# An FFN down projection as one level of Strassen, a finer weight ring and moved seams, in a layer bound by TensorE

## The chip, the cores and the metric

The kernel runs on all 8 cores of one Trainium2 chip (two dies of four cores). Each core computes one batch element of 8192 tokens; the cores exchange nothing. The metric is the device time in microseconds (us) of the slowest core. Such a program has two states, whatever the kernel: in many executions the cores of one die, sometimes of both, show a lower granted TensorE clock, and the time is some per cent to 18% longer. Everything below compares fast executions with fast executions, or undisturbed dies with each other. "Typical core" means the median over the cores of one profiled execution; it is some 10 us below the slowest core.

## The reference

The layer is a macaron: half a SwiGLU FFN, a mixer, half a second FFN, then a final norm. The FFNs hold most of the arithmetic. `D_MODEL` is 1024, `D_FF` is 2816, `SEQ` 8192.

```python
def swiglu_ffn(x, w_gu, w_down):
    gate, up = jnp.split(x @ w_gu, 2, axis=-1)
    return (jax.nn.silu(gate) * up) @ w_down

for l in range(DEPTH):        # DEPTH = 1
    x = x + 0.5 * swiglu_ffn(rms_norm(x, ffn1_norm_g[l]), ffn1_w_gu[l], ffn1_w_down[l])
    x = x + hybrid_mixer(rms_norm(x, mix_norm_g[l]), ...)   # mLSTM branch, pooling branch, gated merge
    x = x + 0.5 * swiglu_ffn(rms_norm(x, ffn2_norm_g[l]), ffn2_w_gu[l], ffn2_w_down[l])
return rms_norm(x, final_norm_g)
```

## The kernel before

The tokens go through in 16 tiles of 512. Step s issues two FFNs, the second FFN of tile s-1 and the first FFN of tile s+1 ("F2" and "F1" below), and weaves the mixer of tile s into them. One such step is called a round. Matmuls are bf16; the activations lie with channels on the partitions and tokens along the free axis. Before the rounds there are three stretches that fill the pipeline: F1 of tile 0, F1 of tile 1 (with the first mixer), F2 of tile 0. I call them the start.

The down projection makes 8 output chunks of 128 channels, each as 22 matmuls of 512 tokens that accumulate in one PSUM bank, and one eviction on VectorE (DVE), which reads the sum from PSUM and adds it to `x`:

```python
def down(j, part):
    def run():
        s = ringF.use(p0 + 11 + j)
        w = wF[s]
        ...
        for k in range(part * 11, part * 11 + 11):
            mm(PS(b), w[:, k * 128:(k + 1) * 128], hid[:, k, :], k == 0, k == NFC - 1)
        if part == 1:
            stt(x[:, j, :], PS(b), 0.5, x[:, j, :], ALU.mult, ALU.add)
            ringF.release()
    return run
```

All weights stream from DRAM for every tile through a ring of four slots of 4096 columns. The first use of a piece comes as fp32 through a casting transfer; the bf16 copy is stored right away to a scratch in DRAM, from the queue of SyncE (SP), and later tiles load that copy:

```python
if k not in converted:
    converted.add(k)
    dma("pool", ch_c[s], w[:, 0:n], wsrc_d[k][:, 0:n], ...)      # fp32 -> bf16 on the way
    ...
    dma("sp", ch_s[s], scr_d[k][:, 0:n], w[:, 0:n], ...)          # keep the bf16 copy
else:
    ...
    dma("sp", ch_w[s], w[:, 0:n], scr_d[k][:, 0:n], ...)
```

The seams between tiles: the final norm of the tile before is put among the first units of the next FFN, and the mixer ends with the norm that feeds the next F2:

```python
un.insert(4 + 2 * q, p)                # final-norm units, from the 4th unit on
...
norm_rs(1, 0, "M")
norm_xn(xnF, x, G2, 0, range(KC))      # eight scalings in one go
...
interleave(main, side, 0.0, 0.95)
```

A small recorder derives every wait from the tiles that an operation reads and writes, so a buffer that is used twice brings its wait with it, and DMAs of one channel wait for each other.

The softmax here doesn't subtract the row's maximum and nothing guards it: scores larger than these inputs give would overflow.

## Time and profile before

| fast executions | us |
|---|---|
| before, 16 executions in all | median 5482.8; the fast ones 5476 to 5484 |
| typical core of the profile | 5469.6 |
| of this: the three stretches of the start | 228.6 + 241.4 + 179.1 (sum on the typical core 647.6) |
| the rounds in the middle (14 F1 and 13 F2) | 4465.8; one round is 174.5 (F1) + 155.5 (F2) = 330.0 |
| the last two F2 | 356.3 |

The stretches are cut where the matmuls pass from the down projection of one FFN to the gate/up projection of the next. The lines of the profile that carry the argument stand in the prediction. How to read it: the tenths show by slices when an engine was busy; the windows show the same in microseconds for chosen stretches; the waits say for whom PE (TensorE) stood still. PE is TensorE (PEld its weight loads), DVE is VectorE, ACT ScalarE, POOL GpSimd, SP SyncE. Of the names, `hid` is the FFN's hidden layer, `x` the residual stream, `xnF` and `xnM` the normalised inputs of FFN and mixer, `accb` the sum of squares for a norm, `ys`, `tF`, `Cf` and `sm` buffers of FFN and mixer, `wF` and `wM` the weight rings, `wsrc` the fp32 weights, `scr` and `scrD` the scratches in DRAM.

### The profile page before, as it was taken

To read this page: it belongs to the slowest core of one execution; us is meant where nothing else is said; L and a number is where in the kernel's file an instruction comes from. 1 tells how busy PE (TensorE), PEld (TensorE's weight loads), DVE (VectorE), ACT (ScalarE), POOL (GpSimd) and SP (SyncE) were. 2 spreads that over 40 slices of the span, in tenths; PEclk is the share of its full clock that TensorE was granted. 3 is DMA by queue.
4 is the path that set the end of the run, shared out by engine and by line. 5 is a ranking of instruction groups with operands and counts; after the bars stand their busy time and mean duration, and the time that the engine had idled before them with its cause. 6 is when DMAs were issued, how large, how long until landed. Compare 5 with 4: busy or idle time off the path is not lost.

```text
span 5481.8 us, 74964 instructions; the slowest of 8 cores (5458.8 to 5481.8 us)
## 1 busy us (share of the span) xinstructions
PE 5262.0 (96%) x25751; PEld 2425.4 (44%) x25751; DVE 2063.0 (38%) x3028; ACT 1694.5 (31%) x2979; POOL 1003.4 (18%) x967
## 2 busy tenths in 40 slices
PE   6688999999999999999999999999999999999998
PEld 2243444444444444444444444444444444444443
DVE  1243424444343343424444243343434434243432
ACT  1223323333232333323333232332423333233322
POOL 0212312112120221202112120221302112120210
PEclk9899999999999999999999999999999999999999
DMA  9969944444434444444544434444444444434433
GB/s 201 216 163 210 223 165 146 173 155 173 158 139 176 153 171 152 151 165 150 179 155 167 156 138 172 157 173 152 146 172 148 176 158 154 169 139 158 151 129 138
DMA packets 145122, 894.89 MB, mean 163 GB/s; under 512 B 16240, under 2 KB 18416, under 8 KB 79600
## 3 DMA queue, kind: packets, MB, share of 16 engines
q1 hardware_dynamic: 136400, 842.07, 43.8%
q0 software_dynamic: 7632, 47.19, 5.6%
q8 instruction: 215, 3.52, 0.3%
q14 instruction: 155, 1.27, 0.1%
q10 hardware_dynamic: 720, 0.84, 0.1%
HBM read 855.43 MB, written 81.79 MB: 171 GB/s over the span
## 4 chain that ended last, share of the span: by engine, by line
PE 81%; DMA 7%; DVE 5%; ACT 3%; issue 3%; POOL 1%; DVEq 0%; ACTq 0%; SPq 0%; POOLq 0%
PE ps L329 80%; DVE xnF L357 3%; DMA wF<-wsrc 2%; ACT L350 2%; DMA scr<-wF 2%; DVE x L357 1%; DMA wM<-wsrc 1%; ACT rs L350 1%; DMA wM<-scr 1%; DMA x<-pb 1%; PE ps L333 0%; POOL accb L353 0%; ACT sqt L350 0%; ACT tM L350 0%; DVE Cf L353 0%
## 5 line engine op out<-in xcount | busy, mean ns | idle before, releaser
L329 PE MATMUL ps<-xnF,wF 128*128 128x512 bf16 x11264 | 2579.1, 380 | 37.5 <-ACT tF L350 13.0
L329 PEld LDWEIGHTS ps<-xnF,wF 128*128 128x128 bf16 x11264 | 1099.1, 98 | 1367.8 <-issue 77.2
L329 PE MATMUL ps<-hid,wF 128*128 128x512 bf16 x5632 | 1270.9, 380 | 38.1 <-DMA wF<-wsrc 38.1
L353 DVE TENSOR_TENSOR hid<-tF,ps 128x512 bf16<-128x512 f32 x704 | 481.5, 686 | 1693.1 <-PE ps L329 1497.7
L329 PE MATMUL ps<-xnM,wM 128*128 128x512 bf16 x4096 | 971.6, 381 | 38.4 <-DVE ys L357 25.8
L353 POOL TENSOR_TENSOR acc<-acc,sqt 128x512 f32<-128x512 f32 x378 | 494.2, 1311 | 2742.7 <-ACT sqt L350 2736.1
L329 PEld LDWEIGHTS ps<-hid,wF 128*128 128x128 bf16 x5632 | 546.2, 98 | 675.0 <-issue 45.2
L350 ACT ACTIVATE tF<-ps 128x512 f32<-128x512 f32 x704 | 418.4, 596 | 1263.5 <-PE ps L329 1210.2
L329 PEld LDWEIGHTS ps<-xnM,wM 128*128 128x128 bf16 x4096 | 401.0, 98 | 521.2 <-issue 49.8
L357 DVE SCALAR_TENSOR_TENSOR x<-ps,x 128x512 f32<-128x512 f32 x384 | 264.6, 689 | 743.4 <-PE ps L329 740.5
L350 ACT ACTIVATE sqt<-x 128x512 f32<-128x512 f32 x441 | 270.0, 625 | 776.1 <-DVE x L357 620.8
L350 ACT ACTIVATE tM<-ps,pvh 128x512 f32<-128x512 f32 x320 | 219.9, 687 | 773.6 <-PE ps L329 773.6
L357 DVE SCALAR_TENSOR_TENSOR tM<-zy,pv_s,tM 128x512 f32<-128x512 bf16 x384 | 294.2, 767 | 197.2 <-POOL tM L365 155.4
L350 ACT ACT_TABLE_LOAD x223 | 286.1, 1283 | 129.8 <-PE ps L329 104.5
L357 DVE SCALAR_TENSOR_TENSOR tB<-tM,ps 128x512 bf16<-128x512 f32 x256 | 176.0, 688 | 239.2 <-PE ps L329 239.1
L357 DVE SCALAR_TENSOR_TENSOR xnF<-x,pv_s,rs 128x512 bf16<-128x512 f32 x256 | 205.1, 867 | 117.9 <-ACT rs L350 117.9
L329 PE MATMUL ps<-qkT,wM 128*128 128x512 bf16 x1024 | 242.7, 381 | 5.4 <-DMA wM<-wsrc 5.4
L365 POOL TENSOR_SCALAR tM<-zy,pv_s 128x512 f32<-128x512 bf16 x128 | 92.8, 728 | 666.3 <-ACT zy L350 607.7
L329 PEld LDWEIGHTS ps<-qkT,wM 128*128 128x128 bf16 x1024 | 100.5, 98 | 127.9 <-issue 8.3
L350 ACT ACTIVATE zy<-ps,pv_s 128x512 bf16<-128x512 f32 x128 | 87.6, 684 | 199.2 <-PE ps L329 199.2
L329 PE MATMUL ps<-wM,xnM 128*128 128x512 bf16 x512 | 122.1, 382 | 13.1 <-DMA wM<-scr 13.1
L329 PE MATMUL ps<-poolT,wM 128*128 128x512 bf16 x512 | 131.4, 379 | 0.0
(82 smaller groups left out, 2244.2 us busy)
## 6 DMA issues: line engine op xcount, KB each, us to landing
wF<-scr SPq DMA_DIRECT2D x330, 1024.0 KB, 4.9
wF<-scr SPq DMA_DIRECT2D x240, 704.0 KB, 4.2
wM<-scr SPq DMA_DIRECT2D x105, 1024.0 KB, 5.9
wM<-scr SPq DMA_DIRECT2D x120, 768.0 KB, 4.5
out<-x SPq DMA_DIRECT2D x64, 512.0 KB, 3.7
x<-x SPq DMA_DIRECT2D x15, 2048.0 KB, 12.7
wF<-wsrc POOLq DMA_DIRECT2D x22, 1024.0 KB, 16.4
scr<-wF SPq DMA_DIRECT2D x22, 1024.0 KB, 15.3
```

Of the source, the lines that this page charges most:

```text
L329: P.op("pe", lambda e: e.matmul(out, lhsT, rhs, start=start, stop=stop), reads=[lhsT, rhs], writes=[out])
L350: P.op("act", lambda e: e.activation(out, in_, func, **kw), reads=rd, writes=wr)
L353: P.op(eng, lambda e: e.tensor_tensor(out, in0, in1, op), reads=[in0, in1], writes=[out])
L357: P.op("dve", lambda e: e.scalar_tensor_tensor(out, in0, scalar, in1, op0, op1), reads=rd, writes=[out])
L365: P.op(eng, lambda e: e.tensor_scalar(out, in0, s1, s2, op0, op1), reads=rd, writes=[out])
```

## The change

The intent is to take arithmetic from PE, which is 96% busy. It has three parts that come together.

1. **Strassen.** The down projection is cut in halves by output chunks (4 and 4), by contraction chunks (11 and 11) and by tokens (256 and 256), and done with seven products, m1 to m7, instead of eight. Most products take sums or differences of quarters of the weights or of `hid` as inputs. DVE makes the token-side sums. The weight-side sums are made once, at tile 0 of each FFN, which itself is computed plainly, and are stored in a new scratch `scrD` that later tiles load.
2. **Ring.** Four slots of 4096 columns become 16 of 1024, so pieces of different sizes follow each other densely. The converted weights of tile 0 are stored after use, no longer right after the cast.
3. **Seams.** The final norm comes 16 units later, the mixer starts 3% later, the eight scalings are spread, two projections of the mixer move behind the mLSTM part, and some buffers are shared to make room.

```diff
-NF = 4
+SUB = 1024
+NSUBF = 16
+PROD = ("m2", "m1", "m5", "m3", "m6", "m4", "m7")
...
-        hid = sb("hid", [128, NFC, T], BF16)
-        wF = [sb(f"wF{i}", [128, 4096], BF16) for i in range(NF)]
+        hid = sb("hid", [128, 5, KH, TH], BF16)      # 4 quarters and one for sums
+        wF = sb("wF", [128, NSUBF * SUB], BF16)
...
+        ch_sF = [P.dma_chan(f"sF{q}") for q in range(4)]
...
+                            if not first:
+                                ringF.release((which, i, "gu", g))
+                                tt(q5(4, g, g + 1), q5(0, g, g + 1), q5(3, g, g + 1), ALU.add)
...
+                def conv_put(n):
+                    ...
+                    for q, pr in enumerate(PROD):
+                        o = st["sum", n, pr]
+                        dma("sp", fch(ch_sF, "s"), scrD_d[...], o, ...)
...
+                EV = {"m1": ((0, 0, 0.5), (1, 1, 0.5)), "m2": ((1, 0, 0.5), (1, 1, -0.5)), "m5": ((0, 1, 0.5), (0, 0, -0.5)),
+                      "m3": ((0, 1, 0.5),), "m6": ((1, 1, 0.5),), "m4": ((1, 0, 0.5),), "m7": ((0, 0, 0.5),)}
+                RHS = {"m2": 0, "m1": 4, "m5": 3, "m3": 4, "m6": 1, "m4": 0, "m7": 2}
+
+                def product(q, pair, mi):
+                    ...
+                        if mi == 0 and pr not in ("m6", "m7"):
+                            st["b", pair] = bank("F")     # m6, m7 accumulate on the bank of m3, m4
+                        b = st["b", pair]
+                        for k in range(KH):
+                            mm(PS(b, mi * TH, (mi + 1) * TH), ringF.col(pc, (mi * KH + k) * 128), hid[:, RHS[pr], k, :], ...)
+                        if mi == 1:
+                            for bot, hf, sc in EV[pr]:
+                                v = xq(4 * bot + 2 * pair, hf)
+                                stt(v, PS(b)..., sc, v, ALU.mult, ALU.add)
...
+                sums = (tsum(4, 1, 3, ALU.subtract) + tsum(1, 0, 1, ALU.add) +
+                        tsum(0, 2, 0, ALU.subtract) + tsum(2, 2, 3, ALU.add))
+                for q in range(7):
+                    for pair in range(2):
+                        for mi in range(2):
+                            down.append((1.2, product(q, pair, mi)))
+                            if q >= 2 and pair == 0 and sums:
+                                down.append((0.0, sums.pop(0)))
...
-            @u(0.3)
-            def _():
-                norm_rs(1, 0, "M")
-                norm_xn(xnF, x, G2, 0, range(KC))
+            us.append((1.5, lambda: norm_rs(1, 0, "M")))
+            for k in range(KC):
+                us.append((0.6, lambda k=k: norm_xn(xnF, x, G2, 0, [k])))
...
-                        un.insert(4 + 2 * q, p)
+                        un.insert(20 + 2 * q, p)
...
-                interleave(main, side, 0.0, 0.95)
+                interleave(main, side, 0.03, 0.95)
```

Cut from the diff: the ring class and its loaders, the sums of the weights at tile 0, the shared buffers, the moved projections and the host's layout of the weights.

## The prediction

> **What bounds the kernel now.** I read the per-core view first, then the head of the page, the chain of waits, PE's waits, the groups by shape, the timeline and the windows. All cores agree within 0.4% at a granted clock of 0.988 to 0.991, so this profile (5481.8 us) is the fast state; the medians of the two dies differ by 10 us. The quoted 5591.58 us is a median over two fast and two slow executions and is not my base: everything below is fast against fast.
>
> ```profile
> span 5481.8 us, 74964 instructions; the slowest of 8 cores (5458.8 to 5481.8 us)
> PE 5262.0 (96%) x25751; PEld 2425.4 (44%) x25751; DVE 2063.0 (38%) x3028; ACT 1694.5 (31%) x2979; POOL 1003.4 (18%) x967
> PE   6688999999999999999999999999999999999998
> DMA  9969944444434444444544434444444444434433
> PE 81%; DMA 7%; DVE 5%; ACT 3%; issue 3%; POOL 1%; DVEq 0%; ACTq 0%; SPq 0%; POOLq 0%
> ```
>
> PE carries the span. DVE has room on average. The first five slices are different: DMA is full there and PE is not.
>
> ```profile
> L329 PE MATMUL ps<-hid,wF 128*128 128x512 bf16 x5632 | 1270.9, 380 | 38.1 <-DMA wF<-wsrc 38.1
> L357 DVE SCALAR_TENSOR_TENSOR x<-ps,x 128x512 f32<-128x512 f32 x384 | 264.6, 689 | 743.4 <-PE ps L329 740.5
> L353 DVE TENSOR_TENSOR qkT<-tB 128x512 bf16<-128x512 bf16 x128 | 54.4, 425 | 14.0 <-DVE tB L357 0.9
> 2639.78 2.54 PE L329 MATMUL ps<-xnF,wF 128*128 128x512 bf16 x11
> 316.27 0.39 PE L329 MATMUL ps<-qkT 128*128 128x128 bf16 x4
> 316.49 0.39 PE L333 MATMUL ps<-cbf,qkT 128*128 128x128 bf16 x4
> ```
>
> The 380 ns is a latency, not a cost: eleven 512-wide matmuls take 2.54 us, so each new one costs (2.54 - 0.38)/10 = 216 ns. Four 128-wide ones start every 0.22 us, 55 to 56 ns each, with new weights every time. Pricing all matmuls of the groups so (23,623 bf16 of 512 columns at 215.8 ns, 1,536 of 128 or 130 at 56.5, the small rest 20 us) gives 5,205 us. The other 277 us is PE waiting or running cold. The windows tell where; I cut them where the timeline passes from hid matmuls to xnF matmuls, which is where one FFN ends.
>
> ```profile
> 0.00:230.60 230.60, 138.42 (x553) 57.44 (x553) 38.52 (x58) 36.06 (x57) 33.88 (x46) 0.87 0.95 211
> 478.80:658.90 180.10, 159.41 (x807) 73.66 (x805) 77.59 (x110) 61.92 (x121) 53.86 (x61) 0.95 0.98 218
> 1648.30:1822.80 174.50, 171.09 (x804) 77.67 (x803) 61.10 (x96) 44.36 (x66) 18.10 (x14) 1.00 0.50 175
> 1822.80:1978.30 155.50, 154.77 (x808) 73.18 (x807) 67.25 (x94) 61.62 (x120) 42.96 (x43) 1.00 0.40 143
> ```
>
> After the span the columns are busy time of PE, weight loads, DVE, ACT, POOL, then granted clock, DMA share, GB/s. Counting the same prices per window: the first FFN holds 108 us of waits, the stretch to 478.8 another 37, the first F2 25; one steady round (both middle rows) is 330.0 us and holds about 5; the last two FFNs 31. So 170 us at the start, some 13 x 5 = 65 us in the steady part, 31 at the end.
>
> ```profile
> PE ps L329 <- DMA wF<-wsrc: 40.5, 5, 17.5
> PE ps L329 <- DVE x L363: 28.7, 3, 25.0
> PE ps L329 <- DVE ys L357: 25.8, 14, 2.3
> PE ps L329 <- POOL accb L353: 15.5, 15, 3.4
> PE ps L329 <- ACT tF L350: 13.4, 15, 1.0
> ```
>
> Waits seen about 15 times are once per round; those seen 3 or 5 times are the start.
>
> **What the Trainium skill says.** (1) "TensorE: Matmul & The Clock Gate", section "Wait — 56ns, not 53.3ns?": a warm stream starts a matmul every N/2.4 ns plus about 2.5 ns. This trace agrees at N = 512 (216) and 128 (56); at N = 256 it gives 109.2 ns, an estimate from that page, as no 256-wide matmul exists here. (2) "VectorE: DVE Perf Modes", "The perf-mode tier table": bf16 tensor_tensor in SBUF makes two elements a cycle, and any fp32 PSUM operand falls to one; its preceding errata section has a fixed term of 151 cycles at 0.96 GHz. The trace agrees: (512/2 + 151)/0.96 = 424 ns against 425, and 689 ns from PSUM. (3) "SBUF — State Buffer", "Who interferes with whom": DVE operations with two SBUF inputs contend with GpSimd operations that read SBUF. The trace has a related sign: the cast Cbf<-Cf takes 431 to 1316 ns for one shape. (4) The first page again, its peak-current warning under "Seeing it yourself": a die of busy cores can be held at 13/16 of the clock. This fast profile doesn't show it; whether it explains the slow executions stays open.
>
> **The change part by part.** The down projection becomes one level of Strassen: halves of 4 output chunks, 11 contraction chunks and 256 tokens, seven products instead of eight. That removes arithmetic from the bound engine.
>
> PE. An FFN's down part was 8 x 22 = 176 matmuls x 215.8 ns = 37.98 us. It becomes 7 x 4 x 11 = 308 of 256 columns x 109.2 ns = 33.63 us. The fixed part eats some of the eighth: 4.35 us is saved instead of 4.75. Tile 0 of each FFN stays plain while it makes the weight combinations, so 30 of 32 FFNs gain: 30 x 4.35 = **-130 us**. All of it is on the path in the steady part.
>
> DVE. Evictions go from 8 to 20 per FFN: 12 x 0.69 = 8.3 us. Four token-side sums of 2816 bf16 columns, each split 1536 + 1280: (768+151)/0.96 + (640+151)/0.96 = 0.96 + 0.82 us, four times = 7.1 us. Eleven sums of 256 columns in the gate/up part: 11 x 0.29 = 3.2 us. Together 18.6 us x 30 = 560 us, plus two sets of weight sums (estimate: 40 sums of 640 or 768 columns, about 0.53 us, 21 us each). DVE goes from 2063 to about 2660 us, half of the span. Not on the path by sum, but it bunches: a product is 44 x 0.109 = 4.8 us of PE, some 7.5 us with mixer work between. Its evictions (up to 4 x 0.69) and one sum (1.8) fill 2.4 to 4.6 us of that before the mixer's own DVE work. Where eight xnF scalings (0.75 each) land in the same stretch, DVE falls behind. Estimate: 0.5 us of PE stall per Strassen FFN, **+15 us**.
>
> DMA. Down weights go from 8 x 704 KB to 14 x 704 KB per FFN: 30 x 4.1 MiB = 130 MB more loads, and 9 MB more stores; 895 becomes about 1030 MB, 194 GB/s. The start already ran at 218 GB/s, and a load lands in 4.2 us with five pieces ahead: hidden in the steady part.
>
> Seams. Final-norm work moves from after the 4th to after the 20th unit; the mixer starts 3% later; the xnF scalings are spread. That should remove the accb wait (1 us a round) and part of the tF, hid and xnF waits (together about 2). The ys wait stays: its transposes still take all four mixer banks, and two pooling outputs now sit between them on DVE. Net **-20 us**.
>
> Start. Stores of converted gate/up weights no longer sit on SP's queue ahead of the pooling matrix, whose load was issued at 52.2 us and cost PE a 25 us wait: most of that goes. Against it, a slot is held until used and stored, and tile 0's down weights need sums on DVE, then 56 small stores per FFN; each sum waits for the previous store to leave the shared scratch. With DMA at 0.95 to 0.98 busy in the first and third windows, I expect -15 in F1 and +10 in F2: **-5 us**. End: xnF earlier, a two-chunk tail instead of one: **-3 us**.
>
> Sum: -130 + 15 - 20 - 5 - 3 = -143; 5481.8 - 143 = 5339, taken as 5335.
>
> **The rivals.** (a) DVE becomes the local bound in the down parts. For: the bunching above, and slowdown beside POOL, whose adds already take 1.3 us; a collision can add about 0.9 us (431 against 1316). Against: 50% on average, four banks that let PE run two products ahead. If each Strassen FFN lost 3 us instead of 0.5, 75 us of the gain goes: 5410. (b) Short matmuls lose to their weight loads. For: twice the loads per column, 98 ns each against 109. Against: 128-wide ones keep 56 ns with such a load each, so the loads overlap. At 120 ns per matmul the saving would be only 1.0 us per FFN: about 5440. (c) The start gets longer: the chain sum, store, sum on tile 0 costs 40 to 60 us more in two DMA-full stretches: about 5385. (d) The seam repairs work fully and the pooling wait goes whole: 65 + 25 us of present waits shrink to 20: about 5285.
>
> **Range and chances.** The PE saving is nearly arithmetic (122 to 141 us at 110 to 108 ns). The start is uncertain by 25 us, the DVE stalls by 25, the seams by 15; together about 38 us. Eight in ten: 5270 to 5410. The 2% line lies at 0.98 x 5481.8 = 5372, one such width above the estimate; (a), (b) and (c) lie beyond it. Faster 0.77, same 0.20, slower 0.03.
>
> **What would show it.** Right: 9,240 hid matmuls of 256 columns starting every 109 ns; a steady round near 320 us instead of 330.0; DVE near 2660 us; no accb wait; no 25 us gap before 84 us; about 1030 MB. Wrong: PE waits on DVE's hid sums or x evictions of over 1 us a round (a); a pace of 115 ns or more (b); the first three windows together above 659 us (c). A round that gets shorter by over 14 us would mean that the seams held more than I counted.

## The result, and the profile after

The changed kernel is correct. Ten executions gave a median of 5498.1 us; the fast ones took 5397 to 5416. The ratio of fast runs is 0.986, with a 95% interval of 0.985 to 0.988: 1.4% faster, which is within the 2% that count as the same. Ratios here are the mean time of one kernel's fast runs over that of the other's of the same rounds, so not quite the ratio of the medians quoted.

The head of the page after (slices as before):

```profile
span 5414.6 us, 86602 instructions; the slowest of 8 cores (5382.4 to 5414.6 us)
PE 5190.3 (96%) x29711; PEld 2826.9 (52%) x29711; DVE 2592.8 (48%) x4038; ACT 1654.2 (31%) x2951; POOL 1029.1 (19%) x988
DMA  9968865565556556455555646556555655655445
```

The page is of core 7, whose clock was 0.979; six of the eight cores ran at 0.985 to 0.987 and ended at 5382 to 5392. (In the clock records of the trace, cores 6 and 7 spent 155 us of the start at 0.8125, and core 4, for one, none; so the 5414.6 is not quite undisturbed, and the typical core is the better measure.) PE is still at 96%, DVE went from 2063 to 2593 us, and the start is as full of DMA as before.

The groups by shape after (busy us, mean ns of one, then idle time before them by cause):

```profile
L405 PE MATMUL ps<-hid,wF 128*128 128x256 bf16 x9240 | 1070.9, 275 | 47.7 <-DVE hid L429 44.0 <-DVE x L433 3.4
L433 DVE SCALAR_TENSOR_TENSOR x<-ps,x 128x512 f32<-128x512 f32 x744 | 513.6, 690 | 538.0 <-PE ps L405 516.9
...
L429 DVE TENSOR_TENSOR hid<-hid 128x1536 bf16<-128x1536 bf16 x120 | 118.9, 991 | 0.0
```

The counts are the ones expected: 9,240 short matmuls, 360 more evictions (744 against 384), 120 of each long sum. The durations of DVE are, too: 991 ns for the 1536 columns, 299 for the 330 short sums of 256 (not shown). What is new is in the first line's tail: PE waits 44 us for the sums that DVE writes into `hid`.

PE's waits after, on core 4 (us in total, times, longest):

```profile
PE ps L405 <- DMA wF<-wsrc: 75.4, 21, 14.8
PE ps L405 <- DVE hid L429: 46.3, 42, 1.9
PE ps L405 <- DVE xnM L433: 17.3, 36, 0.5
...
PE ps L405 <- POOL accb L429: 7.9, 4, 5.7
```

The once-per-round accb wait (15 times before) is down to 4 at the start and the end. In its place stand two waits for DVE, on `hid` 42 times and on `xnM` 36 times, several per round, and more waiting for the casting loads of the start.

The windows after, on core 4: the three stretches of the start, then F1 and F2 of one steady round (columns as in the prediction: span; busy PE, PEld, DVE, ACT, POOL; granted clock; DMA share; GB/s):

```profile
0.00:225.60 225.60, 148.76 (x553) 58.96 (x554) 62.23 (x93) 36.07 (x57) 36.48 (x47) 0.88 0.97 212
225.60:481.10 255.50, 219.61 (x1210) 113.87 (x1211) 117.22 (x186) 73.80 (x138) 48.24 (x55) 0.94 0.77 207
481.10:671.60 190.50, 159.60 (x783) 72.53 (x784) 86.94 (x139) 60.88 (x120) 47.85 (x55) 0.95 0.92 212
992.70:1167.20 174.50, 173.32 (x968) 93.72 (x967) 76.39 (x117) 42.50 (x67) 30.44 (x28) 1.00 0.61 208
1167.20:1314.30 147.10, 144.25 (x908) 83.04 (x907) 84.44 (x133) 60.18 (x119) 31.48 (x31) 1.00 0.52 174
```

The round fell from 330.0 to 321.6 us (322.1 in the median of the cores), all of it in F2; F1 is exactly as long as before, although a Strassen down projection should be 4.35 us shorter. (What the windows of F1 and F2 share between them also depends on where the mixer's units fall, so the round is the better measure.) The second and third stretch of the start are longer than before (248.2 and 180.1 on the same core). Over the whole: the start went from 647.6 to 669.9 us on the typical core, the rounds in the middle from 4465.8 to 4362.8, the end from 356.3 to 354.1; the typical core from 5469.6 to 5386.5.

### The profile page after: what moved, and what is told of

Read it like the earlier page. It is cut to its first block, busy times and chain, and to the rows that moved or that the text cites. A ratio compares the mean times of both kernels' runs of the same rounds, so it can differ in the third digit from the quotient of the medians.

```text
span 5414.6 us, 86602 instructions; the slowest of 8 cores (5382.4 to 5414.6 us)
## 1 busy us (share of the span) xinstructions
PE 5190.3 (96%) x29711; PEld 2826.9 (52%) x29711; DVE 2592.8 (48%) x4038; ACT 1654.2 (31%) x2951; POOL 1029.1 (19%) x988
## 3 DMA queue, kind: packets, MB, share of 16 engines
q14 instruction: 181, 1.48, 0.1%
## 4 chain that ended last, share of the span: by engine, by line
PE 84%; DVE 6%; DMA 5%; issue 2%; ACT 1%; POOL 1%; SPq 0%; DVEq 0%; POOLq 0%; ACTq 0%
PE ps L405 84%; DVE x L433 2%; DMA wF<-wsrc 2%; DVE xnM L433 1%; DVE hid L429 1%; DMA scr<-wF 1%; DVE xnF L433 1%; DMA scrD<-hid 1%; DMA scrD<-wF 1%; DVE Cf L429 1%; DMA wM<-wsrc 1%; DVE tM L433 1%; PE ps L409 0%; ACT rs L426 0%; ACT L426 0%
## 5 line engine op out<-in xcount | busy, mean ns | idle before, releaser
L405 PE MATMUL ps<-xnF,wF 128*128 128x512 bf16 x11264 | 2616.7, 383 | 50.7 <-DMA wF<-wsrc 27.9
L405 PE MATMUL ps<-hid,wF 128*128 128x256 bf16 (+1 forms) x9592 | 1165.3, 280 | 92.8 <-DMA wF<-wsrc 45.1
L405 PEld LDWEIGHTS ps<-hid,wF 128*128 128x128 bf16 x9592 | 939.5, 99 | 311.4 <-issue 139.1
L433 DVE SCALAR_TENSOR_TENSOR x<-ps,x 128x512 f32<-128x512 f32 x744 | 513.6, 690 | 538.0 <-PE ps L405 516.9
L429 DVE TENSOR_TENSOR hid<-hid 128x256 bf16<-128x256 bf16 (+2 forms) x570 | 315.9, 554 | 35.0 <-DVE hid L429 1.2
L433 DVE SCALAR_TENSOR_TENSOR vu<-tM,ps 128x512 bf16<-128x512 f32 x256 | 175.9, 687 | 150.6 <-PE ps L405 149.0
L433 DVE SCALAR_TENSOR_TENSOR xnF<-x,pv_s,rs 128x512 bf16<-128x512 f32 x256 | 186.2, 778 | 8.7 <-ACT rs L426 8.7
L405 PE MATMUL ps<-ys,wM 128*128 128x512 bf16 x512 | 132.4, 380 | 3.2 <-DVE ys L433 2.6
```

The lines of the kernel that those rows point to most:

```text
L405: P.op("pe", lambda e: e.matmul(out, lhsT, rhs, start=start, stop=stop, skip_group_check=more), reads=[lhsT, rhs], writes=[out])
L429: P.op(eng, lambda e: e.tensor_tensor(out, in0, in1, op), reads=[in0, in1], writes=[out])
L433: P.op("dve", lambda e: e.scalar_tensor_tensor(out, in0, scalar, in1, op0, op1), reads=rd, writes=[out])
```

## The experiments

All kernels but one (`seams_only`) are edits of the changed kernel. Sums of stretches below are medians over the cores of one profiled fast execution: start, middle, end. The start scatters: in runs whose edits leave it alone (`m4_first`, `m4_first_b`, `no_tsums`) it took 672.0 to 679.4 us against 669.9, so differences of under 10 us there say nothing.

**What came from which part**

`plain_down` keeps the ring and the seams and takes Strassen out: every tile loads the plain pieces and computes as tile 0 does.

```diff
-                for q in range(7):
-                    for pair in range(2):
-                        ringF.add(Piece((w, i, q, pair), 3, load_down(w, q, pair)))
+                for n in range(8):
+                    ringF.add(Piece((w, i, "dc", n), 4, load_dc(base[w] + 11 + n, n)))
...
-            if first:
+            if True:
```

The sums of tokens and weights go as well; tile 0 stores its plain pieces (`keep_dc`).

> The changed kernel with the down projection left plain in all tiles (176 matmuls of 512 columns, 8 evictions, no sums, no extra stores); ring, seams and mixer order stay as changed. By the sum, the PE part and the DVE waits go together: steady round 326 to 327.5 us. If the start's loss comes from Strassen's weight sums and stores, the first three windows return to about 650 us and the ratio is 0.990 to 0.992; if it comes from the new ring (slots held until used and stored), they stay at about 668 us and the ratio is 0.994 to 0.996.

Measured: 5394.7, 5391.3 and 5392.0 us in its three fastest executions; a fourth, 5451.9, is in the ratio to before of 0.986 [0.978, 0.994]. Typical core 5381.6: start 624.4, middle 4404.6, end 352.4. Windows on core 4:

```profile
0.00:205.40 205.40, 140.80 (x554) 56.98 (x554) 39.35 (x58) 35.42 (x56) 34.23 (x44) 0.91 1.02 209
...
462.30:636.20 173.90, 152.59 (x776) 70.53 (x775) 70.44 (x106) 59.27 (x118) 41.09 (x47) 0.96 0.95 216
961.40:1138.80 177.40, 177.40 (x836) 80.90 (x835) 59.55 (x85) 42.55 (x66) 30.66 (x27) 1.00 0.54 180
1138.80:1286.50 147.70, 147.70 (x775) 70.19 (x774) 66.64 (x103) 59.70 (x118) 29.60 (x31) 1.00 0.44 140
```

This is the most telling run. Without Strassen the kernel is as fast as with it: 5381.6 against 5386.5 us. In both steady rows PE is busy the whole span (177.40 of 177.40, 147.70 of 147.70): the round of 325.1 us has no wait left, and neither has any other round of that core. So ring and seams together bring what the change brings: 23 us at the start, 61 in the middle, 4 at the end. Strassen then takes 42 us from the middle and puts 45 on the start.

`seams_only` goes the other way: the kernel before with three of the seam edits and nothing else.

```diff
-                norm_rs(1, 0, "M")
-                norm_xn(xnF, x, G2, 0, range(KC))
+            us.append((1.5, lambda: norm_rs(1, 0, "M")))
+            for k in range(KC):
+                us.append((0.6, lambda k=k: norm_xn(xnF, x, G2, 0, [k])))
...
-                        un.insert(4 + 2 * q, p)
+                        un.insert(20 + 2 * q, p)
...
-                interleave(main, side, 0.0, 0.95)
+                interleave(main, side, 0.03, 0.95)
```

> The kernel before with three scheduling edits of the change alone (final norm after the 20th unit instead of the 4th, mixer 3% later, xnF scalings one by one). If the seam waits are really removed by the edits, the POOL accb, ACT tF, DVE hid and DVE xnF waits of a round (0.64 + 1.16 + 0.89 us in one round of core 1) go and the ys wait of 2.1 us stays: 14 x 2.7 = 38 us less, ratio to before 0.993. If the waits only move to other places of the round, the ratio is 0.998 to 1.002. No effect on the first 230 us.

Measured: 5448.0 us in its fastest run; most others were slow, so the ratio 0.996 [0.983, 1.010] says little and the trace has to serve. Typical core 5438.9: start 663.1, middle 4423.9, end 351.2. The round is 327.0, so 3.0 us less than before, 42 us over the middle. The rest of the seams' 61 us comes with the parts that were not in this run (moved projections, shared buffers, the ring). Which waits went is not what was expected: between 663 and 5080 us on core 4 the waits for `ys`, `accb` and `hid` are gone, while that for `tF` stays (15.4 us, 13 times). At the start it lost: the third stretch grew from 179.1 to 190.3. One wait of PE on core 4 carries that:

```profile
PE ps L329 <- DMA wM<-scr: 40.8, 6, 25.9
```

Its longest, 25.9 us, lies in that stretch and ends at 553.0 us (before, on the same core: 13.1 at that place). That the order of loads and stores on SP's queue makes it is my reading; I did not test it.

**The waits for DVE in the rounds**

In the changed kernel, the timeline of DVE on core 1 in a down projection of F2 (start, duration, what):

```profile
1923.53 1.78 DVE L429 TENSOR_TENSOR Cf<-Cf,sm 128x520 f32<-128x520 f32 x1
1925.41 1.31 DVE L447 CAST Cbf<-Cf 128x520 bf16<-128x520 f32 x1
1926.64 1.48 DVE L433 SCALAR_TENSOR_TENSOR x<-ps,x 128x512 f32<-128x512 f32 x2
1928.04 0.95 DVE L429 TENSOR_TENSOR hid<-hid 128x1536 bf16<-128x1536 bf16 x1
```

and PE's timeline beside it:

```profile
1929.13 0.81 PE L405 MATMUL ps<-hid,wF 128*128 128x256 bf16 x6 [0.50 <-DVE hid L429]
1931.26 8.92 PE L405 MATMUL ps<-hid,wF 128*128 128x256 bf16 x65 [1.31 <-DVE hid L429]
```

Two operations of the mixer's state take 1.78 and 1.31 us (the fastest of the same shapes 0.70 and 0.43), then two evictions come, and only then the sum that product m3 needs. Beside the two slow ones, POOL's additions for a norm run (1.27 us from 1923.48, 1.48 from 1924.95); that they make them slow was not tested (see the last section). PE starts the first six matmuls late by 0.50 us and the rest, which need the second half of the sum, by another 1.31. The sum cannot come sooner, for it overwrites the fifth quarter of `hid`, which m1 reads.

`sums_early` gives m3 a sixth slot in `hid`, so that the sum can be made one product earlier.

```diff
-        hid = sb("hid", [128, 5, KH, TH], BF16)
+        hid = sb("hid", [128, 6, KH, TH], BF16)
-                RHS = {..., "m3": 4, ...}
+                RHS = {..., "m3": 5, ...}
-                sums = (tsum(4, 1, 3, ALU.subtract) + ...
+                sums = (tsum(5, 1, 3, ALU.subtract) + ...
-                            if q >= 2 and pair == 0 and sums:
+                            if q >= 1 and pair == 0 and sums:
```

> The changed kernel with a sixth quarter buffer of hid, so that the B12-B22 sum has its own place, and all four token-side sums are issued one product earlier. Theory A, the sums come late because DVE has other work queued ahead of them (the waits of m3 and m4 on DVE hid, 44 us in all): the waits vanish, ratio to before falls from 0.986 to 0.978, steady round of 321.6 us to about 318. Theory B, DVE lacks capacity in the down stretches: the wait comes back as waits for evictions (DVE x) or at other products, ratio 0.984 or more. The first three windows (669 us on core 1) do not move in either.

Measured: three fast executions of 5392.3 to 5395.4 us (ratio 0.983 [0.979, 0.987], its interval overlapping that of the change). The profiled one fell with die 0 at a clock of 0.97; on the undisturbed die the middle takes 4342 to 4354 us (the change: 4362.8). PE's waits on core 5:

```profile
PE ps L405 <- DVE x L433: 41.5, 15, 3.1
...
PE ps L405 <- DVE hid L429: 0.2, 1, 0.2
```

The wait for the sum is gone, and most of it has turned into another: m6 now waits, once per round and 2.7 us in most, for the eviction of m3, on whose bank it accumulates. In F1 the repair holds (the window went from 174.5 to 173.1), in F2 the wait only moved. So the sum's buffer was one cause and DVE's queue in F2 another.

`m4_first` puts m4 between m3 and m6, so that the eviction of m3 has a product's time, and issues the last two sums earlier, since m4 now needs its sum sooner; the two edits were not tested apart. It keeps the sixth quarter of `sums_early`, to which this diff stands.

```diff
-PROD = ("m2", "m1", "m5", "m3", "m6", "m4", "m7")
+PROD = ("m2", "m1", "m5", "m3", "m4", "m6", "m7")
...
-                            st["b", pair] = bank("F")
-                        b = st["b", pair]
+                            st[pr, pair] = bank("F")
+                        b = st[{"m6": "m3", "m7": "m4"}.get(pr, pr), pair]
...
-                            if q >= 1 and pair == 0 and sums:
+                            if (q, pair) in ((1, 0), (2, 0), (2, 1), (3, 0)) and sums:
```

> The early sums again, and the order of products m2 m1 m5 m3 m4 m6 m7 in place of m2 m1 m5 m3 m6 m4 m7, so that m6, which adds into m3's bank, comes a whole product after m3. If DVE is only late for a moment in the F2 down part (it ran 2.9 us behind when m6 asked for m3's eviction in the run before), that wait goes and none takes its place: steady round 318.5 us or less, PE waits on DVE x and DVE hid together under 8 us, ratio to before 0.976. If DVE lacks capacity in that stretch, 2 us or more a round appear at another product: ratio 0.981 or more. The start is as in the changed kernel.

Measured: 5360.1 to 5366.3 us in the fast runs, ratio 0.978 [0.975, 0.981], but the result was wrong (relative error 0.90). The norm statistics of the next tile take a bank in rotation, and with the new order this was the bank that still held m3.

`m4_first_b` gives that statistic a bank of the mixer and is otherwise the same.

```diff
-                ahead.append((0.66, lambda: norm_rs(1, 0, "F")))
+                ahead.append((0.66, lambda: norm_rs(1, 0, "M")))
```

> The wrong result of the first try mended: there the next tile's norm sum took, by rotation, the bank in which m3 waited for m6; it now takes a mixer bank. Everything else is equal, so correct, and ratio 0.977 to 0.979; steady round 319 us; PE waits on DVE hid and DVE x together under 8 us. If the extra use of a mixer bank costs waits, the round is 320 us or more.

Measured: correct; 5358.2 and 5363.1 us in the fast runs; too few rounds had fast runs of both kernels for a ratio. Typical core 5351.0: start 676.0, middle 4320.4, end 353.3. The round is 319.0. PE's waits on core 4:

```profile
PE ps L405 <- DVE xnM L433: 16.9, 35, 0.5
...
PE ps L405 <- DVE sm L433: 12.9, 13, 1.1
```

The waits for `hid` (5.8 us left) and for the evictions (2.7) are gone. Two small ones stay: for the norm's scalings of the mixer and for the mixer's small vectors.

`no_tsums` leaves out all four token-side sums of the change and so is wrong (relative error 0.63): it shows what their load on DVE costs.

```diff
-                sums = (tsum(4, 1, 3, ALU.subtract) + tsum(1, 0, 1, ALU.add) +
-                        tsum(0, 2, 0, ALU.subtract) + tsum(2, 2, 3, ALU.add))
+                sums = []
```

> Wrong on purpose: the changed kernel without the four token-side sums in the down part (7.1 us of DVE per FFN); products, evictions and order stay. The waits of m3 and m4 for sums must vanish. If the load of the sums made DVE late, no wait for m3's eviction comes in their place and the round falls to about 318 us. If evictions, mixer work and collisions with POOL alone make it late, m6 waits 1 us or more a round for m3's eviction, as in the run with early sums (2.9 us).

Measured: one fast run, 5345.3 us, typical core 5332.1: start 672.0, middle 4306.5, end 353.6; round 318.0. In the old order of products, the wait of m6 for m3's eviction does not appear (PE waits three times for evictions, 5.6 us in all, on core 4), nor that for the small vectors. So it was the sums in DVE's queue that made the evictions late in `sums_early`, not the order of the products alone. Against the change the middle is 56 us shorter: so much of what DVE costs there is the four sums. The wait for `xnM` stays at 16.9 us even here. It was 2.7 us in `plain_down`, so it belongs to the rest of Strassen's load on DVE or to where the units now fall; this stays open.

**The start**

Strassen's share of the start (45 us by `plain_down`) needed a cause. It lies in the first and third stretch (223.3 and 191.3 us against 199.9 and 170.4 there); the second is as long in both (254.9 and 254.7). Each piece of tile 0's down weights makes seven stores; they go out over four channels, each of which waits for its last store, and the ring's space is held until they are done.

`store_chans` gives the stores 14 channels, `ring20` the ring 20 slots.

```diff
-        ch_sF = [P.dma_chan(f"sF{q}") for q in range(4)]
+        ch_sF = [P.dma_chan(f"sF{q}") for q in range(14)]
```

> The changed kernel with 14 store channels instead of 4 (each channel lets one store be in flight, and tile 0 issues 7 stores per down piece). Theory S, the starting loss is the stores waiting for each other and holding the ring's slots: a down piece of tile 0 takes 7 us instead of 9.8, the first and third windows shrink by about 15 us each, ratio 0.981. Theory R, the ring is too shallow for two casts in flight whatever the stores do: less than 6 us in all, ratio 0.985 to 0.987. The steady rounds do not move.

```diff
-NSUBF = 16
+NSUBF = 20
```

> The changed kernel with a ring of 20 sub-slots instead of 16 (8 KB more per partition), so that three instead of two down pieces of tile 0 with their sums fit (6 slots each). Theory R (too shallow): two casts in flight, a down piece takes 7 us instead of 9.8, first and third windows 10 to 15 us shorter each, ratio 0.981 to 0.982. Theory S (stores waiting for each other) or a DMA limit: under 6 us, ratio 0.985 to 0.987.

Measured: `store_chans` 5400.7 and 5405.8 us in its fast runs (ratio 0.985 [0.981, 0.989]), start 678.6; `ring20` 5396.2 in its one fast run, start 672.5; the change has 669.9. Neither shortens the start. Both theories, too few channels for the stores and too little room in the ring, fell (each tried alone).

`no_puts_f2` stores no sums in F2 and lets F2's later tiles load F1's, so it is wrong (0.34), with equal loads. `no_wsums` makes no sums of the weights and stores plain pieces instead, wrong too (0.59), with equal stores.

```diff
             def load(p):
+                w = "F1"
...
-                    for q, pr in enumerate(PROD):
+                    for q, pr in enumerate(PROD if which == "F1" else ()):
```

> Wrong on purpose: the changed kernel without the 56 stores of F2's combined down weights; F2 then reads F1's. Sums stay. Theory D (the DMA engines are the limit where tile 0 is converted: 10.1 MB of stores at about 2.9 us a MB are 29 us of DMA work): the third window falls from 191 to about 177 us. If the chain of cast, sums and release is the limit: at most 4 us. The first two windows do not move.

```diff
-                        tt(o, A[x0_], A[x1_], op)
-                        st["sum", n, pr] = o
+                        st["sum", n, pr] = A[n2 % 4]
```

> Wrong on purpose: the changed kernel stores plain slices where the weight sums should go, so tile 0 has no sums on DVE and no wait for the shared scratch; the stores and their bytes stay. Theory D (DMA engines): first and third windows within 4 us of 223 and 191. If the chain through DVE and the scratch is the limit: each falls by 10 us or more.

Measured: without F2's stores the third stretch fell from 191.3 to 176.1 us on the typical core (one fast run, 5383.6 us), about what was expected. The first two stretches, which should not have moved, were 5.6 and 3.6 us longer, which shows the scatter. On core 4 the third reads

```profile
488.50:667.00 178.50, 155.77 (x782) 71.70 (x783) 93.85 (x140) 60.44 (x119) 47.58 (x54) 0.96 0.87 188
```

with a DMA share of 0.87 where the change had 0.92. Without the sums nothing moved: 185 to 194 us on the four cores of the undisturbed die (in each of its three runs one die was slow, so it has no fast run). So the stores are what costs there (their transfers, or the ring space that they hold), not the chain of sums on DVE. What the DMA engines carry in the down part of that stretch of the change (queue, packets, MB, share of 16 engines over 66 us, core 1) shows why there was no room:

```profile
q0 software_dynamic: 3886, 5.25, 55.7%
q1 hardware_dynamic: 6114, 7.98, 34.7%
```

The casting loads (q0) alone take over half of all sixteen engines; the plain loads and stores (q1) moved more with 34.7%. A cast costs 0.557 x 66 / 5.25 = 7.0 us per MB written, a plain transfer 0.347 x 66 / 7.98 = 2.9.

If it is the collision with the casting loads, then making sums and stores one tile later should cure it. `late_conv` does that, on top of `m4_first_b`: tile 0 is plain and keeps plain pieces, tile 1 is plain too and makes the sums.

```diff
-            if i == 0:
+            if i < 2:
...
-                    ringF.add(Piece((w, i, "dc", n), 4, load_cast_dc(base[w] + 11 + n, n)))
-                    ringF.add(Piece((w, i, "st", n), 2, None))
+                    ld = load_cast_dc if i == 0 else load_dc
+                    ringF.add(Piece((w, i, "dc", n), 4, ld(base[w] + 11 + n, n)))
+                    if i == 1:
+                        ringF.add(Piece((w, i, "st", n), 2, None))
...
-                        elif n > 0:
-                            conv_put(n - 1)
+                        elif not bot and n > 0:
+                            (keep_dc if first else conv_put)(n - 1)
```

> The same, and tile 1 of each FFN stays plain too and makes the weight sums and their stores, while tile 0 only converts and keeps plain pieces. Theory D (DMA engines are the limit where tile 0 is converted, and have room later): first and third windows as in the plain-down run (about 201 and 170 us instead of 223 and 191), two more plain FFNs cost 2 x 4.35 us, so about 30 us less than the run beside it: ratio 0.971 to 0.973. If the sums and stores cost PE as much in tile 1 as they did in tile 0, the ratio stays at 0.977 to 0.980.

Measured: correct; 5372.7 to 5373.7 us in three fast runs, slower than `m4_first_b` of the same session. The first stretch became 196.1 and the third 182.2, as hoped, but the second, where F1's sums now are, went to 293.0:

```profile
195.30:488.60 293.30, 225.93 (x1058) 101.49 (x1078) 115.90 (x191) 75.89 (x141) 51.54 (x59) 0.91 0.76 198
```

Its DMA share is 0.76, so DMA is not full; yet PE stands still for 67 of 293 us (35 of 257 in `plain_down`). In the first steady round the F2 with sums took 165.6 us on core 4. Against the plain stretches of `plain_down`, 254.7 and 147.7, sums and stores cost 38 and 18 us. The second stretch still casts the mixer's weights; the F2 does not, so even away from casting loads they cost something. The full DMA is not the whole story; the way in which sums, stores and the next load wait for each other costs too.

`late_conv2` moves F1's sums once more, to tile 2, so that they lie in the steady part, and gives the stores 14 channels (the two edits were not tried apart).

```diff
+CONV_TILE = {"F1": 2, "F2": 1}
-        ch_sF = [P.dma_chan(f"sF{q}") for q in range(4)]
+        ch_sF = [P.dma_chan(f"sF{q}") for q in range(14)]
...
-            if i < 2:
+            if i <= CONV_TILE[which]:
```

> The late conversion with two repairs read from its trace: F1 makes its weight sums at tile 2 instead of tile 1, out of the stretch that also converts the mixer's weights (the second window grew to 293 us there), and 14 store channels instead of 4, because at a DMA share of 0.65 the seven stores of a piece still went out in two rounds and held the slots. F2's sums stay at tile 1. If that was the cause: first three windows about 195 + 258 + 180 us, and the two stretches with sums cost 5 to 8 us beyond the 4.35 us of a plain FFN; core spans about 5325 us, ratio to before 0.972 to 0.974. If sums and stores cost PE 15 us or more wherever they stand, the ratio stays at 0.977 to 0.980.

Measured: correct, and the fastest kernel: 5344.4 and 5347.7 us in its two fast runs, against 5476.6, 5482.6 and 5487.1 of the kernel before in the same session. That makes 5346.0 / 5482.1 = 0.975, without an interval, since too few rounds had fast runs of both. Typical core 5337.7: start 621.8, middle 4363.7, end 351.7. Windows on core 4:

```profile
623.40:821.50 198.10, 181.53 (x821) 81.67 (x836) 79.57 (x121) 43.68 (x68) 33.00 (x29) 0.97 0.63 207
821.50:986.60 165.10, 152.84 (x770) 71.09 (x781) 89.73 (x142) 60.83 (x120) 30.66 (x32) 0.98 0.57 185
```

The start is now that of `plain_down`. The two windows with the sums cost 198.1 and 165.1 us; plain ones cost 177.4 and 147.7 in `plain_down`. So 17 to 21 us per FFN remain for making and storing the sums, at a DMA share of 0.57 to 0.63 and with 14 channels; 5 to 8 (beyond the 4.35 of a plain FFN) were expected. The waits of core 4 in these two windows (623.4 to 986.6 us) show two links of the chain:

```profile
PE ps L406 <- DMA wF<-scr: 24.7, 10, 4.3
...
DVE hid L430 <- DMA scrD<-hid: 28.6, 9, 5.7
```

PE waits for the plain pieces that it multiplies with, and DVE waits, before a new sum, for the store of an earlier one to leave the shared scratch in `hid`. That the second makes the first late is argued, not shown: no run gave the sums a second scratch here.

## Why the prediction was right or wrong

The range (5270 to 5410) holds the middle of the fast runs (5405), near its upper end; two, 5411.5 and 5416.2, lie just above it. The favoured outcome, faster by over 2% with a chance of 0.77, did not come. The saving of PE arithmetic, the main term, was right; three terms of the sum were badly sized, two to the bad and one to the good. That the sum still came so near is partly luck: without the 41 us by which the seams beat their term it would have ended above the range. On the typical core the sum reads (negative is time saved; measured terms are differences of the stretches of before, `plain_down` and after):

| term | predicted | measured |
|---|---|---|
| PE arithmetic | -130 for 30 FFNs | pace as predicted; -117 for the 27 FFNs in the middle, by the predicted 4.35 each |
| DVE stalls | +15 | +75 in the middle: 42 saved of 117 |
| seams (with the ring), middle | -20 | -61 |
| start | -5 | +22: -23 from ring and seams, +45 from Strassen |
| end | -3 | -2 |

The middle and the two last terms make -117 + 75 - 61 + 22 - 2 = -83, the measured difference of the typical cores.

- **PE arithmetic: right.** The short matmuls start every 109 ns, in the median of all 9,240, with a tenth to nine tenths between 109 and 110. The estimate from the pace at 512 and 128 columns held, and rival (b), short matmuls that lose to their weight loads, fell. The last FFN, with no mixer beside it, shows the saving directly (core 4; the changed kernel, then `plain_down`): 4.36 us.

```profile
5333.97 33.79 PE L405 MATMUL ps<-hid,wF 128*128 128x256 bf16 x308
...
5336.65 38.15 PE L405 MATMUL ps<-hid,wF 128*128 128x512 bf16 x176
```

- **DVE stalls: the term mis-sized, by a factor of over five.** "0.5 us of PE stall per Strassen FFN" was 75 / 27 = 2.8. (That is a difference of stretches; PE's waits in the middle on core 4 show 41 us for `hid` and 14 for `xnM` of it. The 41 are 3.1 us a round, so the prediction's own sign of being wrong, over 1 us a round, showed.) The prediction named the mechanism (bunching of evictions and sums, collisions beside POOL) and even the size, 3 us, but as rival (a), against which it held an average of 50% and four banks. The runs showed why the banks do not help: the sum for m3 has to wait for m1 to leave the shared quarter, and m6 accumulates on the bank whose eviction it waits for. These are two dependences inside the order of the products, and no free bank loosens them. The first showed in the changed kernel, the second only once the first was gone. `m4_first_b` loosens both, and the middle falls from 4362.8 to 4320.4.
- **Seams: the term mis-sized, by a factor of three.** The prediction counted 65 us of waits in the middle and expected 20 of it back, since the wait for `ys` would stay. That step failed: on core 4 the wait for `ys` fell from 25.8 us in 14 times to 4.9 in 6, none of it in the middle. `plain_down` gets 61 back, and its steady round has no wait. That was rival (d). It means that the present waits were an upper limit on the gain, and the gain reached it.
- **Start: the sign wrong.** "-15 in F1 and +10 in F2" counted two stretches and left out the one between. Measured: -5, +14 and +12 for the three. The pooling matrix no longer makes PE wait (25.0 us before, at most 2.0 after), which is most of the 29 us by which `plain_down`'s first stretch is shorter than that of before; but Strassen's set-up takes 23 us back in the same stretch and costs 21 in the third. The +14 of the second is in `plain_down` too and not in `seams_only` (241.5), so it comes with the ring or with the parts of the seams that only the whole change has; its cause I did not test. Rival (c) named this with the right mechanism (sum, store, sum) in part: in the third stretch `no_wsums` shows that the sums don't matter, `no_puts_f2` that the stores do.
- **DVE's total: right.** 2593 us against 2660; DMA 1034 MB against 1030. Totals told nothing of the stalls.
- **End:** close, but by accident: two Strassen FFNs should have saved 8.7 us there, and the end is 1.7 us longer than that of `plain_down` (354.1 against 352.4). On core 4 the last F2 kept its gain (129.0 against 132.7); the one before, which still has a mixer beside it, became longer (224.9 against 219.7), with waits for DVE (`xnM`, `tM`, `x`, `hid`, `ys`) of 12 us in the last two F2 against 4. A wait of 5.7 us for `accb` at the very end, 5.2 in `plain_down`, is no part of the difference.

The prediction's sign for (c), the first three windows above 659 us, showed too (671.6 on core 4). So rivals (a), (c) and (d) all came true at once; (a) and (c) cost what (d) brought in, and the net of Strassen in this form was nil. Open are the wait for `xnM`, the 17 to 21 us that making the sums costs even in quiet stretches, the second stretch, and the third of `seams_only`.

## What to carry to other kernels

When a change comes as a bundle, build the bundle without its headline part first: here the ring and the seams gave the whole 1.4%, and the part with the fine arithmetic gave nothing until its order and its set-up were repaired. When work is taken from the bound engine by adding dependent small work to another, look at each dependence inside the new order (who overwrites what I still need, whose bank do I accumulate on), not at the other engine's average. And put one-time preparation into stretches where the transfers have room, not into the start where the queues are already full; here it still cost 17 to 21 us per FFN there.

## What the Trainium skill lacked or had wrong

- "TensorE: Matmul & The Clock Gate", "Back-to-back issue gap": it gives about 131 ns (N = 512) and 81 ns (N = 128) for sustained streams of weight load and matmul, and says that N/2.4 + 2.5 holds only for isolated ones. In this kernel's steady streams, with a new weight load for every matmul, the pace was 216 ns at 512 columns, 109 at 256 and 56 at 128, so the formula held, as the section of the page that the prediction cites has it for back-to-back matmuls, and the figures for sustained streams did not.
- The same page, the warning on the peak-current limiter under "Seeing it yourself": it says that a die goes to 13/16 of the clock soon after its third core starts dense matmuls, stays there while the load lasts, and that 13/16 is to be budgeted for sustained dense matmuls on all cores. That value is what the slow executions show, which the prediction had left open: in `no_wsums` core 0 ran at 0.81 from 712 to 1094 us (its F1 and F2 took 208.7 and 173.3 us there, 173.5 and 148.6 on core 4 of the other die), and its clock records hold 1.0, 0.5 and 0.8125 alone. But under the same load all eight cores held a mean of 0.98 to 0.99 in the fast executions, and core 0 of `no_wsums` was back at 1.00 from 3200 to 4000 us. So three busy cores are not enough to bring it; what decides is open.
- "SBUF — State Buffer", "Who interferes with whom": it states that a DVE operation with two SBUF inputs contends with GpSimd reads, and that a cast can contend when it runs in a two-port mode; its examples of size are 6.8 times for DVE and 1.5 for GpSimd, by who comes first. Nothing there says what to expect of a mixed kernel. Here, on core 1 of the changed kernel, DVE operations of one shape ranged from 0.70 to 1.80 us (128x520 fp32 product) and from 0.43 to 1.32 us (its cast), so 2.6 and 3.1 times. All 13 long casts of that core overlap an addition of POOL in time and none of the 51 short ones does, which agrees with the page; but on core 4 of `plain_down` 13 short casts overlap one too, and no run moved POOL's work, so that POOL is the cause is not shown.
- "DMA: Bandwidth & Descriptors", "SWDGE vs HWDGE vs iDMA": it says which queues can cast, and I found no cost of it there. Here a cast from fp32 to bf16 took 7.0 us of all sixteen engines per MB written against 2.9 for a plain transfer, which is about 3.5 per MB read.
